# Four groups of lag products in a state-space decoder layer: from one PSUM partition range in two banks to four ranges in one bank

## The chip, the core and the metric

The kernel is one program on one core of a Trainium2 chip. The metric is the device time of one execution in microseconds (us). The engines are TensorE (PE; its weight loads are shown apart as PEld), VectorE (DVE), ScalarE (ACT), GpSimd (POOL) and SyncE (SP, which only issues transfers here). SBUF is the working memory and PSUM the memory that TensorE writes its products to; both have 128 partitions, and a PSUM bank holds 512 fp32 numbers in each partition.

## What is computed

The input is one sequence of 1024 positions with 1024 channels, all in fp32. One layer does this:

```python
xn = rmsnorm(h, norm_gain);  proj = xn @ w_in                 # 1024 x 3072
u, z_ssm, h_conv, b_conv, c_conv, z_conv = split of proj in six times 512 columns
# state-space mixer: 32 groups of 16 channels, each drives a complex diagonal state of 64
s[t] = ab * s[t-1] + bb @ u[t];   y = Re(c @ s) + d_skip * u    # per group
y = gelu(y);  y = y * sigmoid(y @ w_glu + b_glu);  y_ssm = y * silu(z_ssm)
# short convolution mixer
y_conv = b_conv * causal_conv3(c_conv * h_conv) * silu(z_conv)
out = rmsnorm(x + concat(y_ssm, y_conv) @ w_out)
```

The kernel doesn't scan position by position. It cuts the sequence into 128 chunks of 8 positions (`C` chunks of `T` positions). What an input adds to an output of the same chunk depends only on how many positions lie between them, the lag 0 to 7. For each group the kernel therefore needs eight 16x16 matrices, one for each lag: c times the state matrix to the power of the lag times bb. These are the lags within a chunk, and the change is about the products that make them.

## The kernel before

Work on the state-space mixer goes in four blocks of eight groups (`G` = 8 groups, `H` = 16 channels, 64 complex states as 128 partitions). The string `ORDER` (line 36) gives the order in which the steps are written: for block n, `p` prepares tables (`ssm_prep`), `m` turns the injection matrix (`ssm_inject`), `q` makes the lags (`ssm_lags`), `i` takes the inputs in and runs the scan over chunks (`ssm_in`), `o` makes the outputs (`ssm_out`). A bare number is half of a convolution product (`conv_hc`, `conv_bz`), which are large products that TensorE can do at any time. `ssm_in` is written under high priority. From this written order, from priorities and from its own estimates, a scheduler at build time fixes one order for each engine; nothing changes place at run time. What TensorE does here, in the order of the trace, is `ps_w` (line 531, eight transposes), the first part of `ps_k` (line 544), all of `ps_s` (line 569), the rest of `ps_k`, then convolution products (`mm_...`, line 230).

The lags of a block, `ssm_lags`, are eight products, one per group: the stationary operand is `bb` of the group (128 states x 16 channels), the moving operand is `vv` of the group (128 states x 128 columns, which are 8 lags x 16 channels), and the result is 16 x 128. Each product is fp32 by fp32, and the trace shows two weight loads and two matmul records for it, called two passes below. Four products fill one PSUM bank (tile `ps_k`, 16 partitions x 4 x 128); then one ACT copy of 16 x 512 (line 546) empties it into `kp` in SBUF. A block has two such tiles and two such copies. DVE adds the skip term to lag 0 (line 550), and eight transfers (line 553) spread `kp` into a block-Toeplitz tile `tp`, with which `ps_y` (line 593) is made much later.

The PSUM tiles of the mixer all come from one pool of four banks (`psm`, line 68): per block two for `ps_w`, two for `ps_k`, two for `ps_s`, two for `ps_y`. A new tile waits until one of the four is empty. The large products use another pool (`pmm`), also of four banks.

On SP, the transfers of line 553 stand in one queue with the loads of the convolution weights (line 111) and with the other transfers; a transfer whose data isn't ready holds up those behind it.

Of the kernel before, what the change touches and what calls it, by code (L numbers as in the profile page):

```python
# [10 lines left out]
F32 = mybir.dt.float32  # L11
# [8 lines left out]
P = 128  # L20
D = 1024
L = 1024
T = 8
# [5 lines left out]
H = 16  # L29
# [28 lines left out]
def hybrid_kernel(ctx: ExitStack, tc, x, norm_gain, w_in, a_re, a_im, log_dt, b_re, b_im,  # L58
                  c_re, c_im, d_skip, w_glu, b_glu, conv_w, w_out, final_gain, out):
    nc = tc.nc  # L60
    V, A, Q, PE = nc.vector, nc.scalar, nc.gpsimd, nc.tensor
# [6 lines left out]
    psm = ctx.enter_context(tc.tile_pool(name="psm", bufs=4, space=PSUM))  # L68
# [323 lines left out]
    bb = par.tile([P, NG, H], F32, name="bb")  # L392
# [31 lines left out]
    with tc.manual_schedule(engines={mybir.EngineType.PE, mybir.EngineType.Activation, mybir.EngineType.DVE}):  # L424
        for what in START.split():
# [10 lines left out]
            elif what[0] == "c":  # L436
                ps = pmm.tile([P, KT], F32, tag="mm", name="ps_g1")
# [97 lines left out]
    def ssm_lags(b, prep):  # L535

        g0 = b * G
        gs = slice(g0, g0 + G)
        vv, ee, rr = prep
        kp = ssm.tile([H, G, T, H], F32, tag="kp", name=f"kp{b}")  # L540
        for q in range(2):
            ps = psm.tile([H, 4, P], F32, tag="sm", name=f"ps_k{b}{q}")
            for g in range(4):
                PE.matmul(ps[:, g], bb[:, g0 + 4 * q + g], vv[:, 4 * q + g, 0:T].rearrange("p t h -> p (t h)"),  # L544
                          start=True, stop=True)
            A.copy(kp[:, 4 * q:4 * q + 4], ps.rearrange("p g (t h) -> p g t h", h=H))
        dd = ssm.tile([H, G, H], F32, tag="dd", name=f"dd{b}")
        V.tensor_tensor(dd, dT[:, gs].unsqueeze(2).to_broadcast([H, G, H]),
                        ident[0:H, 0:H].unsqueeze(1).to_broadcast([H, G, H]), MUL)
        V.tensor_tensor(kp[:, :, 0], kp[:, :, 0], dd, ADD)  # L550
        tp = toep[b % 2]
        for j in range(T):
            nc.sync.dma_start(tp[H * j:H * j + H, :, H * j:P], kp.rearrange("p g t h -> p g (t h)")[:, :, 0:P - H * j])
        return tp
# [90 lines left out]
    for what in ORDER.split():  # L645
        n = int(what.lstrip("pmiqoz"))
        if what[0] == "p":
            prep[n] = ssm_prep(n)
        elif what[0] == "m":
            inj[n] = ssm_inject(n, prep[n])  # L650
        elif what[0] == "q":
            lags[n] = ssm_lags(n, prep[n])
        elif what[0] == "i":
            with tc.high_priority():
                st[n] = ssm_in(n, prep[n], inj[n])
        elif what[0] == "o":
            ssm_out(n, prep[n], lags[n], st[n])
        else:
            (conv_bz if n & 2 else conv_hc)(n // 4, n % 2)
# [273 lines left out]
```

## Time and profile before

| what | value |
|---|---|
| median of 3 runs | 432.88 us (431.73 to 433.24) |
| the profiled execution's own time | 432.44 us |
| its span, first to last instruction | 430.7 us |
| granted TensorE clock, mean | 0.992 |
| matmuls and weight loads | 2226 of each |
| ACT instructions | 323 |
| records of `ps_k`: matmul, weight load, copy | 64, 64, 8 |

An execution's own time is longer than its span by what lies around the first and last instruction, 1.7 us here. In a row of the chain of waits stand start, length, engine, tile and line, and how many instructions were merged (`x10`). In a row of a line's or tile's view stand the count, the shortest, median and longest duration in ns, and the shapes as out<-in. A shape `128*16` on a TensorE row says how many rows and columns of the array the instruction uses.

### The profile page before, as it was taken

How to read it: one execution, taken by the hardware profiler on the slowest of the kernel's cores; microseconds unless marked ns; L12 is line 12 of the kernel's file. 1: busy time of each engine (PE TensorE's matmuls, PEld its weight loads, DVE VectorE, ACT ScalarE, POOL GpSimd, SP SyncE). 2: the span in 40 equal slices, each digit the busy share in tenths (PEclk: the TensorE clock that was granted, in tenths of full speed). 3: DMA queues.
4: the chain of work that ended last, by engine and by line, in shares of the span. 5: the costliest groups of instructions: out<-in, count | busy, mean ns of one | idle time of the engine just before them, and what ended most of it. 6: DMA issues, size and time to landing. Idle time of an engine off the chain costs nothing.

```text
span 430.7 us, 6302 instructions
## 1 busy us (share of the span) xinstructions
PE 418.2 (97%) x2226; PEld 358.0 (83%) x2226; DVE 330.1 (77%) x820; ACT 182.5 (42%) x323; POOL 34.6 (8%) x41
## 2 busy tenths in 40 slices
PE   8998999999999999999999999999999999999992
PEld 7898999888888888888888888888888888888881
DVE  4973888869998999986996928747366799978644
ACT  5754933163313255036224415647434664333113
POOL 0000003000020020100021000211102100000022
PEclk9999989999999999999999999999999999999998
DMA  8883004523170552264025421578444450233212
GB/s 256 251 244 81 20 2 137 157 76 122 18 201 5 148 146 60 64 157 138 7 46 139 127 82 68 180 201 252 108 121 73 131 138 1 99 109 136 97 49 98
DMA packets 49471, 48.96 MB, mean 114 GB/s; under 512 B 6696, under 2 KB 39488, under 8 KB 49440
## 3 DMA queue, kind: packets, MB, share of 16 engines
q1 hardware_dynamic: 47712, 45.42, 35.6%
q0 software_dynamic: 1728, 3.15, 4.2%
q8 instruction: 17, 0.28, 0.3%
q14 instruction: 14, 0.11, 0.1%
HBM read 31.65 MB, written 8.39 MB: 93 GB/s over the span
## 4 chain that ended last, share of the span: by engine, by line
PE 95%; DMA 2%; DVE 1%; ACT 1%; issue 1%; SPq 1%; ACTq 0%
PE mm_u L230 11%; PE mm_b L230 10%; PE mm_h L230 10%; PE mm_z L230 10%; PE mm_c L230 10%; PE mm_zs L230 10%; PE ow L819 10%; PE oz L819 5%; PE glu L747 5%; PE ox L819 3%; PE ps_s L569 2%; PE ps_k L544 2%; PE ps_y L593 2%; DMA wru<-in_w_in_dram 2%; PE ps_y L594 2%; PE ps_x L211 1%
## 5 line engine op out<-in xcount | busy, mean ns | idle before, releaser
L641 POOL TENSOR_TENSOR cy<-cy,sg 128x512 f32<-128x512 f32 x8 | 13.8, 1729 | 185.5 <-DVE sg L640 152.8
L826 ACT ACTIVATE sq<-xr 128x512 f32<-128x512 f32 (+1 forms) x17 | 10.3, 605 | 38.7 <-DVE xr L823 27.2
L747 PE MATMUL glu<-shl,wg 128*128 128x512 f32 x96 | 21.9, 389 | 0.0
L747 PEld LDWEIGHTS glu<-shl,wg 128*128 128x128 f32 x96 | 18.0, 188 | 3.7
L224 DVE SCALAR_TENSOR_TENSOR xl<-ps_x,g,xh 128x256 fp32r<-128x256 f32 x32 | 12.9, 476 | 8.5 <-ACT xh L218 8.5
L230 PE MATMUL mm_u<-xh,whu 128*128 128x256 f32 x128 | 17.5, 288 | 1.7 <-ACT xh L218 1.7
L230 PE MATMUL mm_u<-xl,whu 128*128 128x256 f32 x128 | 18.3, 293 | 0.0
L230 PE MATMUL mm_u<-xh,wlu 128*128 128x256 f32 x128 | 18.3, 289 | 0.0
L230 PEld LDWEIGHTS mm_u<-xh,whu 128*128 128x128 f32 x128 | 16.2, 191 | 2.4 <-ACT xh L218 2.2
L819 PE MATMUL ow<-bs,ax 128*128 128x512 f32 (+1 forms) x54 | 16.9, 367 | 0.5 <-DVE xr L823 0.5
L230 PEld LDWEIGHTS mm_u<-xl,whu 128*128 128x128 f32 x128 | 16.9, 200 | 0.1
L230 PEld LDWEIGHTS mm_u<-xh,wlu 128*128 128x128 f32 x128 | 16.8, 197 | 0.1
L230 PE MATMUL mm_b<-xh,whb 128*128 128x512 f32 x64 | 16.6, 398 | 0.0
L230 PE MATMUL mm_h<-xh,wlh 128*128 128x512 f32 x64 | 16.2, 393 | 0.0
L230 PE MATMUL mm_h<-xh,whh 128*128 128x512 f32 x64 | 16.1, 391 | 0.0
L230 PE MATMUL mm_b<-xl,whb 128*128 128x512 f32 x64 | 15.9, 390 | 0.0
L230 PE MATMUL mm_h<-xl,whh 128*128 128x512 f32 x64 | 15.8, 389 | 0.0
L230 PE MATMUL mm_c<-xh,whc 128*128 128x512 f32 x64 | 15.8, 389 | 0.0
L230 PE MATMUL mm_z<-xh,wlz 128*128 128x512 f32 x64 | 15.8, 389 | 0.0
L230 PE MATMUL mm_c<-xl,whc 128*128 128x512 f32 x64 | 15.8, 389 | 0.0
L230 PE MATMUL mm_z<-xl,whz 128*128 128x512 f32 x64 | 15.8, 389 | 0.0
L230 PE MATMUL mm_zs<-xh,wlzs 128*128 128x512 f32 x64 | 15.8, 389 | 0.0
(354 smaller groups left out, 1108.4 us busy)
## 6 DMA issues: line engine op xcount, KB each, us to landing
ee<-ec SPq DMA_DIRECT2D x16, 256.0 KB
wro<-in_w_out_dram SPq DMA_DIRECT2D x8, 512.0 KB
xr<-in_x_dram SPq DMA_DIRECT2D x8, 512.0 KB
out_dram<-xr SPq DMA_DIRECT2D x7, 512.0 KB
x<-in_x_dram SPq DMA_DIRECT2D x6, 512.0 KB
wrh<-in_w_in_dram SPq DMA_DIRECT2D x4, 512.0 KB
wrc<-in_w_in_dram SPq DMA_DIRECT2D x4, 512.0 KB
uscr<-us SPq DMA_DIRECT2D x32, 64.0 KB
```

The source lines that it names most:

```text
L211: PE.transpose(pss[kt // 2][:, kt % 2, j], x_t[2 * pair + j][:, kt * P:(kt + 1) * P], ident)
L224: V.scalar_tensor_tensor(xl[pair // 2][:, kt, n], ps, g1[:, kt:kt + 1], hs.bitcast(F32), MUL, SUB)
L230: PE.matmul(ps[:, n], a[:, kt], b[half][:, kt, n], start=what == "h" and kt == 0, stop=last and kt == KT - 1)
L544: PE.matmul(ps[:, g], bb[:, g0 + 4 * q + g], vv[:, 4 * q + g, 0:T].rearrange("p t h -> p (t h)"), start=True, stop=True)
L569: PE.matmul(ps[:, g - 4 * q], w1[:, g], u2[:, g], start=True, stop=True)
L593: PE.matmul(ps[:, k], tp[:, g], u2[:, g], start=True, stop=False)
L594: PE.matmul(ps[:, k, 1:C], vv[:, g, 1:T + 1].rearrange("p t h -> p (t h)"), xa[:, g, 0:C - 1], start=False, stop=True)
L641: Q.tensor_tensor(yb[:, n], yb[:, n], sg, MUL)
L747: PE.matmul(ps, wg[:, a, k, es], shl[half][:, y, k], start=m + k == 0, stop=m == 2 and k == NB - 1)
L819: PE.matmul(out_, aq[op_a, j][:, p, k], bq[op_b, k][:, q, cols], start=first and m + k == 0, stop=m == 2 and k == NB - 1, skip_group_check ...
L826: A.activation(temp(f"sq{final_square.n}")[:, 0:x.shape[-1]], x, AF.Square, accum_out=acc)
```

## The change

In `ssm_lags` one PSUM tile of 128 partitions x 2 x 128 takes the place of two tiles of 16 partitions x 4 x 128. Product number 4q + k of the block writes partitions 32k to 32k + 15, part q. The order of the eight products is the same, and so are their operands. Four ACT copies of 16 x 256, one for each partition range, take the place of two copies of 16 x 512; they come after all eight products in the code. `kp` has the same contents in the same places, so that nothing behind it changes.

```diff
         kp = ssm.tile([H, G, T, H], F32, tag="kp", name=f"kp{b}")
+
+        ps = psm.tile([P, 2, P], F32, tag="sm", name=f"ps_k{b}")
         for q in range(2):
-            ps = psm.tile([H, 4, P], F32, tag="sm", name=f"ps_k{b}{q}")
-            for g in range(4):
-                PE.matmul(ps[:, g], bb[:, g0 + 4 * q + g], vv[:, 4 * q + g, 0:T].rearrange("p t h -> p (t h)"),
-                          start=True, stop=True)
-            A.copy(kp[:, 4 * q:4 * q + 4], ps.rearrange("p g (t h) -> p g t h", h=H))
+            for k in range(4):
+                g = 4 * q + k
+                PE.matmul(ps[32 * k:32 * k + H, q], bb[:, g0 + g], vv[:, g, 0:T].rearrange("p t h -> p (t h)"), start=True, stop=True)
+        for k in range(4):
+            A.copy(kp.rearrange("p (q k) t h -> p k q (t h)", k=4)[:, k], ps[32 * k:32 * k + H])
```

## The prediction

> **What bounds the kernel now.** I read the page's busy times first, then its chain of the work that ended last, then the list of TensorE's waits.
>
> ```profile
> span 430.7 us, 6302 instructions
> PE 418.2 (97%) x2226; PEld 358.0 (83%) x2226; DVE 330.1 (77%) x820; ACT 182.5 (42%) x323; POOL 34.6 (8%) x41
> PE 95%; DMA 2%; DVE 1%; ACT 1%; issue 1%; SPq 1%; ACTq 0%
> PE ow L819 <- DVE xr L823: 0.5, 1, 0.5
> ```
>
> TensorE is busy 97% of the span and carries 95% of the chain. The last row is the whole list of TensorE's waits from 100 us to the end: one wait of 0.5 us, close to the end. So whatever TensorE no longer does between 100 and 260 us, where the lags are, comes off the end, as long as nothing new makes it wait.
>
> Then the place itself. The chain, cut to the block that starts near 156 us, lists TensorE's work piece by piece:
>
> ```profile
> 155.78 0.23 PE mm_z L230
> 156.01 0.87 PE ps_w L531 x8
> 156.88 1.19 PE ps_k L544 x10
> 158.08 1.98 PE ps_s L569 x16
> 160.06 0.76 PE ps_k L544 x6
> 160.82 0.43 PE mm_b L230
> ```
>
> The lags stand on the path in two pieces, ten passes and six, with `ps_s` between them. They take 1.19 + 0.76 = 1.95 us a block, 7.8 us over four. That is all that there is to win. The two pieces also give the price of a pass: four passes more cost 1.19 - 0.76 = 0.43 us, so a pass costs 0.108 us, and each piece carries about 0.11 us beside its passes (1.19 - 10 x 0.108). I read the latter as the price of going from the full array to the narrow form or back.
>
> What sets 0.108 us? The view of the line, and two fine cuts of the timeline:
>
> ```profile
> L544 PEld LDWEIGHTS ps_k<-vv,bb x64: 92/97/97, 104.6 to 236.7; 128*16 128x16 f32 x64
> L544 PE MATMUL ps_k<-vv,bb x64: 269/273/283, 104.6 to 236.8; 128*16 128x128 f32 x64
> 156.81 0.11 PEld L544 LDWEIGHTS ps_k<-vv,bb 128*16 128x16 f32 x2 [0.17 <-issue]
> 156.81 0.39 PE L544 MATMUL ps_k<-vv,bb 128*16 128x128 f32 x2
> 156.93 0.10 PEld L544 LDWEIGHTS ps_k<-vv,bb 128*16 128x16 f32 x1
> 150.57 5.44 PE mm_z L230 x24
> ```
>
> A record lasts 0.273 us but the next starts 0.108 us later, so passes are pipelined and it is the streaming of 128 columns that is paid. The full products stream 512 columns in 5.44/24 = 0.227 us, 0.44 ns a column; a lag pass takes 0.108/128 = 0.84 ns a column, so it draws its moving data at half the rate that the array is seen to take. Two weight loads of some 0.095 us each together occupy 0.11 us: the second starts some 0.015 us behind the first. The third starts only at 156.93, when the second matmul has started: a load runs one ahead. The narrow form (`128*16`) leaves 112 of 128 array columns without work.
>
> **The change part by part.**
>
> *Where the products land.* Order, operands and count are as before: 16 passes a block. What is new is that neighbours in the queue use different columns of the array. The trace of before has no two products in different columns, so whether they run at the same time isn't shown, and I bound it. The one end: not at all, and a pass stays at 0.108 us, a gain of nothing. The other end: all passes start at the spacing of the two weight loads, 0.015 us; then each of 9 + 5 followers in the two pieces saves 0.093 us, 1.30 us a block, 5.2 us in all. I take a value between, from the order of the queue: the two passes of one product use the same columns and the same place in PSUM, so the second must wait for the first, but the first pass of the next product may start beside it. Ten passes of five products then take six steps instead of ten, six passes of three products four instead of six. That is 4 + 2 = 6 overlaps of 0.093 us, 0.56 us a block, and **2.2 us** over four. Two streams at half rate also ask for no more moving data than one full-rate product does.
>
> By the Trainium skill's page "TensorE: Matmul & The Clock Gate", Part 3 (measured speedup), three column tiles ran 2.38 times as fast as in a row, with starts about 4 ns apart and in strict queue order; by 4 ns instead of 15 the six overlaps would be an estimated 2.5 us over four blocks. No row here shows columns packed.
>
> *The switch.* Both pieces are narrow before and after, so the two entries and two exits stay. If the scheduler no longer splits the block, because `ps_k` takes one bank less, one piece remains with seven overlaps and one switch price of 0.11 us goes: 0.65 + 0.11 = 0.76 us a block, 3.0 us in all. I don't count on it: the eight products have the same length and order for the scheduler, and `ps_s` waits for the same copies.
>
> *One bank less.* In the last block the pool is tight:
>
> ```profile
> 232.19 0.70 PE mm_h L230 x3
> 232.89 0.11 issue
> 233.00 1.25 PE ps_k L544 x10
> 234.25 2.07 PE ps_s L569 x16
> ```
>
> `ps_s` takes 2.07 us there against 1.98 above. I put the 0.09 us down to its second bank, which must first be emptied by the copy of `ps_k`; with one bank less in use it goes. The 0.11 us ahead of `ps_k` I put down to the output tile `ps_y`, which DVE empties late; that order stays, and I leave it in. Sum: 2.2 + 0.1 = 2.3 us.
>
> *Four copies for two.* ACT's rows for these copies, the nearest row for a copy of 256 numbers out of PSUM, and what stands behind:
>
> ```profile
> L277 ACT ACTIVATE b<-ps_cb x2: 384/384/384, 60.4 to 61.2; 128x256 f32<-128x256 f32 x2
> 157.90 0.57 ACT L546 COPY kp<-ps_k 16x512 f32<-16x512 f32 x1 [0.23 <-PE ps_k L544]
> 161.03 0.59 ACT L571 ACTIVATE xb<-ps_s 64x512 f32<-64x512 f32 x1
> 161.65 0.58 ACT L546 COPY kp<-ps_k 16x512 f32<-16x512 f32 x1
> 164.72 1.06 ACT L105 CAST whb<-wrb 128x1024 fp32r<-128x1024 f32 x1 [2.50 <-PE mm_b L230]
> 166.98 0.27 DVE L550 TENSOR_TENSOR kp<-kp,dd 16x128 f32<-16x128 f32 x1
> 237.82 0.58 ACT L546 COPY kp<-ps_k 16x512 f32<-16x512 f32 x1
> 238.47 0.59 ACT L616 COPY hs<-mm_h 128x512 f32<-128x512 f32 x1
> 241.50 0.28 DVE L550 TENSOR_TENSOR kp<-kp,dd 16x128 f32<-16x128 f32 x1
> ```
>
> Four copies at up to 0.384 us are 1.54 us against 1.15: ACT gets 0.4 us more a block, and it is 42% busy. But no copy can now run before the last product, so where 0.58 us followed the second piece, 1.54 follow: `kp` is complete up to 0.96 us later. Behind them on ACT stands the cast of 164.72, which waited 2.50 us for TensorE: covered. `kp` itself is awaited by DVE's L550, which ran 166.98 - 162.23 = 4.75 us after the copy's end here and 3.1 us in the last block, held by the scan ahead of it in DVE's order; the eight transfers on SP and the weight loads behind them wait for L550 and not for the copies. In the last block L616 stands directly behind and moves by some 0.9 us; it feeds DVE's convolution work, and TensorE has four other banks. I cost the copies at nothing. If the cover were gone, they would cost at most 0.96 us a block, 3.8 us.
>
> The Trainium skill's page "TensorEngine Tiling (Array Packing)", section PSUM Bottleneck, speaks against the change: packing speeds TensorE, not the emptying of PSUM, which may become the bound. The trace doesn't bear that out for these copies, by the 2.50 us of idle time above.
>
> *Does the rest follow?* TensorE gets up to 2 us ahead by the last block. DVE must come along:
>
> ```profile
> 100.00:156.00 56.00, 56.00 (x283) 46.82 (x283) 53.14 (x118) 17.07 (x25) 3.62 (x2) 1.00 0.40 103
> 156.00:198.00 42.00, 42.00 (x225) 35.35 (x222) 36.60 (x76) 15.92 (x25) 3.62 (x2) 1.00 0.38 108
> 230.24 0.43 DVE L599 TENSOR_SCALAR ysb<-ysb 128x512 f32<-128x512 f32 x1 [1.03 <-ACT ysb L598]
> ```
>
> In these stretches (length, PE, PEld, DVE, ACT, POOL) DVE idles 2.9 us of 56 and 5.4 of 42, more than the 0.6 us that TensorE gains in each, and at 230 us it waited 1.03 us for work that TensorE releases.
>
> The sum against the profiled execution: 432.44 - 2.3 = 430.1 us. That execution lies 0.44 us under the median of 432.88, so I forecast 430.6 us for the median, 0.5% less.
>
> **The rivals.**
>
> *No overlap.* If the load of the next product's weights may only start once the matmul ahead of it has started, as the third load at 156.93 did, its first pass comes 0.097 us behind instead of beside: 6 x 0.011 us a block, 0.3 us in all, 432.6 us. For it speaks that loads run only one ahead in every row here; against it that the columns of the next product are idle until then. The change would then not do what it is laid out for. The Trainium skill's page "TensorE: Matmul & The Clock Gate", Part 3, says that loads overlap running matmuls only when the row groups differ; all four groups use 128 rows. Taken strictly, it would mean no overlap here; the trace disagrees in so far as the load at 156.93 runs beside a matmul on the same rows.
>
> *All overlap.* If the two passes of one product also run together, 5.2 us go: 427.6 us. Against it speaks the shared accumulator.
>
> *Slower: each change of columns is a switch.* If a step to another column range drains the array as the switch of form does, 0.11 us is paid at each of 4 + 2 changes inside the two pieces: 0.66 us a block, 2.6 us, 435.5 us. It decides from the first pair on; with a drain there is no overlap to set against it. For it speaks that every change of form in these rows costs 0.11 us; against it that the form stays `128*16`. The Trainium skill's page "TensorEngine Tiling (Array Packing)", section Tiling Modes, says that changing the mode drains and changing the tile alone doesn't, which is against this rival; no run here shows it.
>
> **How the numbers follow.** Overlap of neighbours, split or not: 0.50. All overlap: 0.07. No overlap: 0.30. Slower: 0.13, with a loss of cover at the copies counted in. The range of 8 in 10 leaves out the slower case and most of the full overlap: 428.3 us, past the unsplit case, to 433.3, no overlap plus the spread of the runs. Under the forecast alone it is 429.5 to 431.5. A measurement can tell about 0.3%, 1.3 us, from no change: faster is nearly all of the first two cases, 0.55; same is no overlap and a remainder, 0.32; slower 0.13.
>
> **What would show it.** Right: ten `ps_k` passes in about 0.65 us and six in about 0.46, starts in pairs, with the records' length kept; TensorE's total shorter by 2 us; four copies of about 0.37 us behind `ps_s`; the `ps_s` of the last block at 1.98 us. Wrong: starts still 0.108 us apart (no overlap), gaps of 0.2 us at changes of columns (slower), or a new wait of TensorE on ACT or DVE near 232 us.

## The result

The changed kernel takes 428.91 us in the median (427.74 to 429.41), the kernel before it 433.03 us beside it; the ratio is 0.9907, with a 95% interval from 0.9878 to 0.9936. Measured twice more it was 0.9914 (0.9901 to 0.9928) and 0.9902 (0.9879 to 0.9926). So about 4.1 us went, 0.9%, and not the 2.3 us that the sum gave: right way, in the range, and the gain nearly twice as large.

The page of the changed kernel, its busy times and the chain that ended last:

```profile
span 427.5 us, 6316 instructions
PE 414.7 (97%) x2226; PEld 355.2 (83%) x2226; DVE 333.3 (78%) x820; ACT 183.5 (43%) x331; POOL 36.5 (9%) x41
PE 94%; DMA 2%; DVE 1%; ACT 1%; issue 1%; SPq 1%; ACTq 0%
```

TensorE is still what carries the chain, with the same 2226 matmuls and 3.5 us less busy time; ACT has eight instructions more and 1.0 us more.

The two spans differ by only 3.2 us. The beginning accounts for the rest; the same piece of the chain, before and after:

```profile
3.42 7.13 DMA wru<-in_w_in_dram
103.83 0.87 PE ps_w L531 x8
```

```profile
3.42 8.06 DMA wru<-in_w_in_dram
104.96 0.87 PE ps_w L531 x8
```

The first weights landed 0.93 us later in the profiled execution after, and the first block of the mixer began 1.13 us later; nothing of the change has run by then. From that point to the end it is 430.7 - 103.83 = 326.87 us before and 427.5 - 104.96 = 322.54 us after: 4.3 us less, all of it behind the place of the change.

The chain of the changed kernel in its first and in its last block (start, length, engine, tile and line; line 546 is `ps_k`, 571 is `ps_s`):

```profile
104.96 0.87 PE ps_w L531 x8
105.83 0.32 PE ps_k L546 x2
106.15 2.02 PE ps_s L571 x16
108.17 0.55 PE ps_k L546 x14
...
232.30 0.11 issue
232.41 0.38 PE ps_k L546 x2
232.79 1.98 PE ps_s L571 x16
234.77 0.55 PE ps_k L546 x14
```

Two things are new. Fourteen passes take 0.55 us where ten took 1.19: they no longer cost 0.108 us each. And the block is cut after one product instead of five, so the pieces are 2 and 14 passes and not 10 and 6. The first three blocks take 0.87 us each and the last 0.93, 3.54 us in all; before they took 1.96, 1.95, 1.96 and 2.01, 7.88 us. That is 4.34 us less.

The records of single passes are as long as before (the profiler models where a matmul's record ends, so the starts tell more); what has changed is when the next one starts. From the view of the tile:

```profile
L546 PE MATMUL ps_k<-vv,bb x64: 269/273/283, 105.8 to 235.1; 128*16 128x128 f32 x64
L548 ACT COPY kp<-ps_k x16: 340/364/368, 109.8 to 237.6; 16x256 f32<-16x256 f32 x16
```

And a fine cut of the timeline, the first 0.025 us of a second piece (start, length of the merged instructions):

```profile
108.10 0.12 PEld L546 LDWEIGHTS ps_k<-vv,bb 128*16 128x16 f32 x6
108.10 0.30 PE L546 MATMUL ps_k<-vv,bb 128*16 128x128 f32 x4
```

A record still lasts 0.273 us, but four matmuls lie within 0.30 us, so they start within 0.03 us of each other, and six weight loads lie within 0.12 us. Start by start, the trace has the first four passes 0.006 to 0.007 us apart, then nothing for 0.10 us, then the next four: the fourteen passes come in rounds of 4, 4, 3 and 3. I read a round as one pass in each range of columns, so four products at once; the runs below bear that out.

### The profile page after: what moved, and what is told of

Its sections match the earlier page's. It is cut to its first block, busy times and chain, and to the rows that moved or that the text cites. A ratio compares the mean times of both kernels' runs of the same rounds, so it can differ in the third digit from the quotient of the medians.

```text
span 427.5 us, 6316 instructions
## 1 busy us (share of the span) xinstructions
PE 414.7 (97%) x2226; PEld 355.2 (83%) x2226; DVE 333.3 (78%) x820; ACT 183.5 (43%) x331; POOL 36.5 (9%) x41
## 4 chain that ended last, share of the span: by engine, by line
PE 94%; DMA 2%; DVE 1%; ACT 1%; issue 1%; SPq 1%; ACTq 0%
PE mm_u L230 11%; PE mm_b L230 10%; PE mm_c L230 10%; PE mm_h L230 10%; PE mm_z L230 10%; PE mm_zs L230 10%; PE ow L821 10%; PE glu L749 5%; PE oz L821 5%; PE ox L821 3%; DMA wru<-in_w_in_dram 2%; PE ps_s L571 2%; PE ps_y L595 2%; PE ps_y L596 2%; PE ps_x L211 1%; PE ps_cb L275 1%
## 5 line engine op out<-in xcount | busy, mean ns | idle before, releaser
L643 POOL TENSOR_TENSOR cy<-cy,sg 128x512 f32<-128x512 f32 x8 | 16.1, 2015 | 179.2 <-DVE sg L642 146.9
L230 PE MATMUL mm_b<-xh,wlb 128*128 128x512 f32 x64 | 15.9, 391 | 0.0
L230 PE MATMUL mm_zs<-xh,whzs 128*128 128x512 f32 x64 | 15.8, 389 | 0.0
L230 PE MATMUL mm_zs<-xl,whzs 128*128 128x512 f32 x64 | 15.8, 389 | 0.0
```

What stands on the lines that cost most here:

```text
L230: PE.matmul(ps[:, n], a[:, kt], b[half][:, kt, n], start=what == "h" and kt == 0, stop=last and kt == KT - 1)
L643: Q.tensor_tensor(yb[:, n], yb[:, n], sg, MUL)
```

## The experiments

I held this theory: **columns side by side**. Each range of columns works through its own passes 0.109 us apart, the ranges run beside each other, and a piece lasts 0.109 us times the passes of its busiest range, plus about 0.1 us for the switch of form. It has three rivals: that the freed bank and the new order made the gain; that only next neighbours in the queue overlap, as the forecast had it; and that the copies give part of it back. Each diff below is against the changed kernel.

**Packed, but in two banks.**

```diff
-        ps = psm.tile([P, 2, P], F32, tag="sm", name=f"ps_k{b}")
         for q in range(2):
+            ps = psm.tile([P, P], F32, tag="sm", name=f"ps_k{b}{q}")
             for k in range(4):
                 g = 4 * q + k
-                PE.matmul(ps[32 * k:32 * k + H, q], bb[:, g0 + g], vv[:, g, 0:T].rearrange("p t h -> p (t h)"), start=True, stop=True)
-        for k in range(4):
-            A.copy(kp.rearrange("p (q k) t h -> p k q (t h)", k=4)[:, k], ps[32 * k:32 * k + H])
+                PE.matmul(ps[32 * k:32 * k + H], bb[:, g0 + g], vv[:, g, 0:T].rearrange("p t h -> p (t h)"), start=True, stop=True)
+            for k in range(4):
+                A.copy(kp[:, 4 * q + k].rearrange("p t h -> p (t h)"), ps[32 * k:32 * k + H])
```

> Four partition ranges as in the change, but two tiles in two banks again (four products each) and a copy per product, eight of 16 x 128 per block. The written order for TensorE goes back to five products, ps_s, three products, as before the change. If the gain comes from products in different columns running side by side (theory: a piece lasts 0.109 us times the passes of its busiest column range, plus about 0.1 us for the switch), the pieces last 4 x 0.109 + 0.1 = 0.54 and 2 x 0.109 + 0.1 = 0.32 us, 0.87 us a block against 1.95 before, and the time is that of the change, about 429 us. If the gain comes from the freed bank and the new order (rival), it is back at about 433 us.

Measured: 429.46 us, ratio 0.9927 (0.9901 to 0.9952). Its chain in the first block:

```profile
105.53 0.54 PE ps_k L546 x10
106.07 1.98 PE ps_s L571 x16
108.05 0.34 PE ps_k L546 x6
```

The pieces are those of before the change, 10 and 6, with the two banks of before, and they take 0.54 and 0.34 us against 1.20 and 0.76. The gain is there without the freed bank and without the new order. The cut after one product is seen with the single bank (the next kernel has it too), and it isn't what pays. What the second bank seems to cost is little: the first piece of the second block and `ps_s` of the last block take longer here than in the first block, and with one bank neither does.

```profile
156.62 0.71 PE ps_k L546 x10
...
232.71 2.11 PE ps_s L571 x16
```

**Two ranges instead of four.**

```diff
-        ps = psm.tile([P, 2, P], F32, tag="sm", name=f"ps_k{b}")
-        for q in range(2):
-            for k in range(4):
-                g = 4 * q + k
-                PE.matmul(ps[32 * k:32 * k + H, q], bb[:, g0 + g], vv[:, g, 0:T].rearrange("p t h -> p (t h)"), start=True, stop=True)
-        for k in range(4):
-            A.copy(kp.rearrange("p (q k) t h -> p k q (t h)", k=4)[:, k], ps[32 * k:32 * k + H])
+        ps = psm.tile([P, 4, P], F32, tag="sm", name=f"ps_k{b}")
+        for q in range(4):
+            for k in range(2):
+                g = 2 * q + k
+                PE.matmul(ps[64 * k:64 * k + H, q], bb[:, g0 + g], vv[:, g, 0:T].rearrange("p t h -> p (t h)"), start=True, stop=True)
+        for k in range(2):
+            A.copy(kp.rearrange("p (q k) t h -> p k q (t h)", k=2)[:, k], ps[64 * k:64 * k + H])
```

> One bank, but only two partition ranges (0 and 64) with four products each, and two copies of 16 x 512 as before the change. By the theory of columns side by side the seven products of the second piece have eight passes in the busier range: 8 x 0.109 + 0.1 = 0.98 us, with 0.31 us for the first piece 1.29 us a block against 1.95 before and 0.9 with the change: about 430.5 us. If the bank and the order make the gain (rival), about 429 us; if only next neighbours in the queue can overlap (the forecast's model), seven products take 8 steps too, so this run does not tell that apart, but the change itself would then take as long as this one.

Measured: 430.83 us, ratio 0.9948 (0.9932 to 0.9964).

```profile
105.55 0.32 PE ps_k L546 x2
105.87 2.02 PE ps_s L571 x16
107.89 0.98 PE ps_k L546 x14
```

One bank and the same order as the change, but the fourteen passes take 0.98 us, as 8 x 0.109 and about 0.1 say, against 0.55 with four ranges. Half the ranges bring a good half of the gain, 2.3 us. The two ACT copies are those of before, so the number of copies isn't what limits it either.

**One range, all in one piece.**

```diff
-        ps = psm.tile([P, 2, P], F32, tag="sm", name=f"ps_k{b}")
         for q in range(2):
+            ps = psm.tile([P, 4, P], F32, tag="sm", name=f"ps_k{b}{q}")
             for k in range(4):
                 g = 4 * q + k
-                PE.matmul(ps[32 * k:32 * k + H, q], bb[:, g0 + g], vv[:, g, 0:T].rearrange("p t h -> p (t h)"), start=True, stop=True)
-        for k in range(4):
-            A.copy(kp.rearrange("p (q k) t h -> p k q (t h)", k=4)[:, k], ps[32 * k:32 * k + H])
+                PE.matmul(ps[32:32 + H, k], bb[:, g0 + g], vv[:, g, 0:T].rearrange("p t h -> p (t h)"), start=True, stop=True)
+            A.copy(kp[:, 4 * q:4 * q + 4], ps[32:32 + H].rearrange("p g (t h) -> p g t h", h=H))
```

> All eight products in partitions 32 to 47, two banks, two copies of 16 x 512: nothing is side by side, and the order on TensorE happens to put all eight products into one piece. Theory of columns: 16 x 0.109 + 0.1 = 1.85 us a block, 0.1 us less than before for the one switch saved: about 432.6 us, no measurable gain. Rival of the order (an undivided piece is what counts): about 430 us or less.

Measured: 432.40 us, ratio 0.9990 (0.9971 to 1.0008), no difference from before.

```profile
105.53 1.85 PE ps_k L546 x16
107.38 0.43 PE mm_b L230
107.81 1.78 PE ps_s L570 x16
```

Sixteen passes take the 1.85 us of 16 x 0.109 + 0.1 (in the last block they stand in two pieces of eight). In one range the starts stay about 0.109 us apart. Another place in PSUM and an undivided piece alone bring nothing that can be measured.

**Neighbours in the queue share columns.**

```diff
-        for q in range(2):
-            for k in range(4):
+        for k in range(4):
+            for q in range(2):
                 g = 4 * q + k
```

> The change with the products written range by range (0, 0, 32, 32, 64, 64, 96, 96), so that neighbours in the queue share columns; nothing else moves. If TensorE can take passes of other columns from behind one that waits, the seven products of the second piece again take 4 rounds, 0.55 us. If a pass that waits holds up all behind it, only the three steps from one range to the next overlap: 14 - 3 = 11 rounds, 1.3 us a piece, 3 us in all.

Measured: 427.31 us, in a single execution; the reading is of the trace and not of this time. Its chain:

```profile
105.82 0.57 PE ps_k L546 x14
```

A fine cut of its timeline, the first 0.045 us of that piece:

```profile
105.75 0.32 PE L546 MATMUL ps_k<-vv,bb 128*16 128x128 f32 x4
```

Fourteen passes take 0.57 us, not 1.3, and four matmuls again lie within 0.32 us. With this order a strict queue could have started only one of the first four passes, since the others in front share its range or stand behind one that waits. So passes for other columns start ahead of one that waits. A rival would be that the scheduler gave TensorE the products in another order than the written one. The starts speak against it: they are about 0.007, 0.013 and 0.013 us apart here, in all four blocks, against steps of 0.006 to 0.007 us in the changed kernel. The written order of this piece is one product for the first range, then two for each of the others, so the longer steps stand just where a product of the same range has to be passed over. This fits the written order without proving it. (By what means it happens, whether the array takes passes from behind in the queue, each range has a queue of its own, or the two passes of a product are put apart before they are queued, the trace does not tell; for the time it is the same.) Unless the passes are put apart beforehand, the sentence on the kernel before, that nothing changes place at run time, doesn't hold for them.

**Eight copies for four.**

```diff
-        for k in range(4):
-            A.copy(kp.rearrange("p (q k) t h -> p k q (t h)", k=4)[:, k], ps[32 * k:32 * k + H])
+        for q in range(2):
+            for k in range(4):
+                A.copy(kp[:, 4 * q + k].rearrange("p t h -> p (t h)"), ps[32 * k:32 * k + H, q])
```

> The change with eight copies of 16 x 128 in the place of four of 16 x 256. TensorE's order is the same. At 0.26 us a copy ACT gets 2.1 us a block instead of 1.45, and kp is complete 0.6 us later. If the copies lie beside other work (forecast), the time is that of the change, within 0.3%. If they are on the path (rival), 0.6 us a block are added: 2.5 us, about 431.5 us.

Measured: 429.44 us, ratio 0.9925 (0.9913 to 0.9938). The changed kernel itself, on the same chip:

> The changed kernel once more, beside the next three on the same chip: about 429 us. Its lags take 0.86 to 0.97 us a block in two pieces of 2 and 14 passes, 3.6 us in all.

It took 428.91 us, ratio 0.9914 (0.9901 to 0.9928). The difference of 0.5 us is below 0.3% and the intervals overlap; the 2.5 us of the rival are excluded. The copies lie beside other work where the change puts them.

**The lags behind `ssm_in`.** If a piece costs four rounds whether it holds seven products or eight, the first piece of 0.32 us is lost. In `ORDER` each `q` goes behind its `i`:

```diff
-ORDER = "p0 0 1 2 m0 q0 i0 3 p1 4 5 o0 6 m1 q1 i1 7 p2 8 o1 9 m2 q2 i2 10 p3 11 o2 m3 q3 i3 12 13 o3 14 15"
+ORDER = "p0 0 1 2 m0 i0 q0 3 p1 4 5 o0 6 m1 i1 q1 7 p2 8 o1 9 m2 i2 q2 10 p3 11 o2 m3 i3 q3 12 13 o3 14 15"
```

> The change with the lags written behind ssm_in instead of ahead of it, so that all eight products of a block stand in one piece behind ps_s, and a convolution product fills the wait of ps_s for its copy. Theory of columns side by side: 4 rounds of 0.109 and about 0.12 us for the switch and the steps, 0.55 us a block instead of 0.86 to 0.97: 2.2 us in all instead of 3.6, 1.4 us less than the change, about 427.5 us. Rival (what the lags save is given back, since kp and the transfers behind it come later and ps_y or the weights then wait): no better than the change, with a new wait of TensorE at ps_y or at a convolution product.

Measured: 427.94 us, ratio 0.9886 (0.9868 to 0.9903). It is the fastest of the kernels that were timed in several rounds, 1.0 us under the change beside it; the intervals just touch, so the step from the change is likely rather than certain. Its second block, from the chain:

```profile
155.57 0.58 ACT sg L641
156.15 0.48 ACT w L532
156.63 0.04 issue
156.68 2.05 PE ps_s L571 x16
158.73 0.56 PE ps_k L546 x16
```

Sixteen passes in 0.56 us, as expected. But ahead of `ps_s` the chain goes over ACT: `ps_s` waits 0.4 us for the copy of `ps_w`, which stands behind a sigmoid (line 641). Before the change 1.2 us of lag passes lay there and covered this. It isn't the new place that does it: the changed kernel beside it has the same wait in the same block, 0.6 us.

```profile
PE ps_s L571 <- ACT w L532: 0.6, 1, 0.6
```

**The lags ahead of `ssm_inject`.**

```diff
-ORDER = "p0 0 1 2 m0 q0 i0 3 p1 4 5 o0 6 m1 q1 i1 7 p2 8 o1 9 m2 q2 i2 10 p3 11 o2 m3 q3 i3 12 13 o3 14 15"
+ORDER = "p0 0 1 2 q0 m0 i0 3 p1 4 5 o0 6 q1 m1 i1 7 p2 8 o1 9 q2 m2 i2 10 p3 11 o2 q3 m3 i3 12 13 o3 14 15"
```

> The same with the lags written ahead of ssm_inject: one piece of eight products ahead of ps_w, and kp complete earlier. Theory: 0.55 us a block as well, about 427.5 us; against lags_last only the place differs. Rival: the pieces of ps_w and ps_s that now stand apart cost more than the merged piece saves, about 429 us.

Measured: 430.66 us, ratio 0.9954 (0.9936 to 0.9973), 1.7 us slower than the change. The chain in its first block:

```profile
104.42 0.67 PE ps_k L546 x16
...
105.16 0.36 ACT kp L548
...
106.28 0.37 ACT kp L548
106.65 0.02 issue
106.68 0.59 ACT ysb L532
107.27 0.04 issue
107.31 2.05 PE ps_s L571 x16
```

Here the four copies are on the path: ACT takes them one after the other, 1.5 us, ahead of the copy for which `ps_s` waits. The list of TensorE's waits in this kernel has three new ones:

```profile
PE ps_s L571 <- ACT w L532: 1.7, 2, 1.4
PE ps_s L571 <- ACT ysb L532: 0.6, 2, 0.3
PE ps_k L546 <- DVE vv L505: 0.8, 1, 0.8
```

The expectation was missed, and the rival named another cause. Behind the copies `ps_s` waits about 0.3 us in each of the first three blocks, and in the first the lags themselves wait 0.8 us for the table that DVE makes. The longest wait, 1.4 us, is that of the last block and has another cause. On ACT:

```profile
225.48 1.49 ACT L548 COPY kp<-ps_k 16x256 f32<-16x256 f32 x4
228.24 0.63 ACT L603 ACTIVATE ysb<-ysb 128x512 f32<-128x512 f32 x1 [1.26 <-DVE ysb L602]
228.89 1.07 ACT L532 COPY w<-ps_w 128x512 f32<-128x512 f32 x2
```

The four copies are over at 226.97, and ACT stands idle for 1.26 us. What comes ahead of the copy of `ps_w` there is a step of the output tile (line 603), which waits for DVE. So the place of the copies makes about 0.9 us of the 3.1 us of these waits.

**`ps_s` tied behind the last lag product**, so that all eight cover its wait (`last_lag[b]` is the last lag product of the block; the lines that note it are left out here):

```diff
-                PE.matmul(ps[:, g - 4 * q], w1[:, g], u2[:, g], start=True, stop=True)
+                with tc.issue_after(last_lag[b]):
+                    PE.matmul(ps[:, g - 4 * q], w1[:, g], u2[:, g], start=True, stop=True)
```

> The change with ps_s tied behind the last lag product in TensorE's order, so that the order is ps_w, all eight lag products, ps_s. One piece of 4 rounds, 0.56 us a block, and it lies in the time in which ps_s would wait for the copies of ps_w on ACT. Theory of columns side by side, with ps_s's wait for ACT as what is late next: 2.2 us for the lags in all instead of 3.6, waits of ps_s under 0.1 us a block: 427.5 us, and less than lags_last by what ps_s waited there. Rival: the later ps_s makes the scan chain and so ps_y late, no better than the change.

Measured: 430.85 us, ratio 0.9949 (0.9931 to 0.9967); the change beside it:

> The changed kernel beside the run before on the same chip: about 429 us.

It took 429.25 us, ratio 0.9902 (0.9879 to 0.9926). The expectation was missed, by what happens from the last block on. The first block in the chain:

```profile
103.85 0.56 PE ps_k L546 x16
104.41 1.98 PE ps_s L572 x16
```

And the longest of TensorE's waits:

```profile
PE ps_s L572 <- DVE ysb L605: 2.6, 1, 2.6
```

In the first three blocks it is as meant: 0.56 us and no wait. In the last block `ps_s` waits 2.6 us for a bank that the output tile of the block before holds until DVE has read it (line 605). In this order the last block also stands earlier: its `ps_w` starts at 221.8 us, against 228.4 us in the change beside it. Whether the tie or the earlier place makes the bank late was not tried apart.

The wait isn't all that is lost there. In three stretches of the same execution (length, PE, PEld, DVE, ACT and POOL, then the granted clock):

```profile
226.00:228.00 2.00, 0.00 (x0) 0.00 (x0) 1.90 (x5) 1.26 (x4) 0.00 (x0) 1.00 0.34 79
229.00:230.00 1.00, 1.00 (x6) 1.00 (x6) 0.00 (x0) 0.98 (x2) 0.00 (x0) 0.50 0.94 188
232.00:233.00 1.00, 1.00 (x6) 0.84 (x5) 0.93 (x3) 0.00 (x0) 0.00 (x0) 1.00 1.02 336
```

After the wait the granted clock is 0.50, for 3.4 us (228.54 to 231.96), and convolution products there start up to 0.43 us apart instead of 0.227. Half of 3.4 us, 1.7 us, is an estimate of the loss. The profiled execution of the change beside it has no such stretch near its last block. That the wait brought the slow clock is likely and not shown.

## Why the prediction came out as it did

**The bound: right.** TensorE carried the chain, and what it no longer did came off the end: 4.3 us in the chain from the first block on, 4.1 us in the median.

**The price of a pass and of a switch: right.** 0.108 us and about 0.11 us, read from two pieces of before, give the pieces of all these kernels within 0.03 us once the number of rounds is known, where TensorE goes on without a wait: 0.32, 0.34, 0.54, 0.55, 0.57, 0.98, 1.85 us.

**The overlap: right that there is one, wrong in how far it goes.** The step that failed is "the second must wait for the first, but the first pass of the next product may start beside it. Ten passes of five products then take six steps instead of ten". It took the queue to be strict. The second pass of a product does wait, but it doesn't hold up the products behind it: all four ranges run at once, and a round of four passes costs what one did. The term was 2.2 us and measured 4.34 us (7.88 to 3.54). The rival "all overlap" gave 5.2 us and was too large, since passes in the same columns do stay 0.109 us apart, as the run with two ranges shows. Both bounds were needed, and the truth lay nearer to the far one than the value that I took. That the time fell into the range is in part luck: its lower end, 428.3 us, was set past neighbours that overlap in one unsplit piece, and no case in the prediction had four products at once with the passes of each one apart. The two signs named for being right don't follow from the sum either: by its own terms ten passes should take 1.19 - 4 x 0.093 = 0.82 us and six 0.76 - 2 x 0.093 = 0.57, not 0.65 and 0.46.

**"No overlap" and "each change of columns is a switch": wrong.** The load of the next weights doesn't wait for the matmul ahead when the columns differ (six loads in 0.12 us), and starts 0.007 us apart leave no room for a drain of 0.11 us.

**The switch and the order: wrong, without weight.** I expected the cut between the fifth and the sixth product to stay, and it moved behind the first. The run with two banks, which has the old cut, costs the same within its interval.

**One bank less: right.** `ps_s` in the last block went from 2.07 to 1.98 us, and with two banks again it takes 2.11 us.

**The copies: right, and with their condition.** Four copies of 0.364 us lie beside other work; with them ahead of the copies of `ps_w`, they were on the path in three blocks.

**What was missed.** The lag passes between `ps_w` and `ps_s` were also a cover: `ps_s` needs the copies of `ps_w` from ACT. With 0.32 us there instead of 1.20, `ps_s` waits a little: 2.02 us in the first block against 1.98, and in the second block the chain of the changed kernel has

```profile
157.29 0.03 issue
157.32 2.05 PE ps_s L571 x16
```

which is 0.10 us more than before; 0.14 us in all. This varies from one execution to the next: in a second profile of the same kernel that block waits 0.6 us, in a third 0.1 us again. For the first profile the sum of the parts is 4.34 + 0.09 - 0.14 = 4.29 us, against 4.33 in the chain.

## What to carry to other kernels

Where TensorE bounds and a product uses few columns of the array, write its neighbours to different 32-partition ranges of PSUM: here four ranges ran as one, and the count to make is the passes of the busiest range, not the instructions. Then look at what the longer products had covered: a wait that nobody saw, here for ACT's copies, is what is late next. And keep the additional copies out of the queue ahead of anything that TensorE waits for. If a kernel with a new wait loses more than the wait, read the granted clock behind it.

## What the runs showed of the hardware

Products in four column ranges start 0.007 us apart and run beside each other although each uses all 128 rows and fp32 operands in two passes. A pass that waits for its own columns doesn't stop passes of later products for other columns: with the products written range by range, fourteen passes took 0.57 us, against the 1.3 us that a strict queue would take at 0.109 us a pass. Passes in one range stay 0.109 us apart: sixteen took 1.85 us. Weight loads, one ahead in the single range, run up to six in 0.12 us over four ranges. After 2.6 us without work for TensorE one run had a granted clock of 0.50 for 3.4 us; after 1.4 us another kept 1.00.
